# Two-layer diffusion step on one core: the first norm's loads and sums in another order, the next layer's adaLN sums held behind the second norm, a scratch tile of its own for the second layer's first norm, value weights in the key tiles' slots

## The chip, the cores and the metric

The kernel runs on one core of a Trainium2 chip. The metric is the device time of one execution in microseconds (us). Three timed runs of the kernel before gave a median of 1824.09 us (1818.67 to 1829.79). Smaller is better.

## The reference

One inference step of a two-layer flow-matching backbone on 128 context tokens and 512 latent tokens of width 1024. For each layer and each of the two token streams:

```
shift, scale, gate (x2) = SiLU(cond) @ w_ada[l] + b_ada[l]     # "adaLN": 6 x 1024 values per stream
h = rmsnorm(x, g_mix) * (1 + scale) + shift                    # first norm
p = h @ w_in[l]     # 14 x 128 columns of queries, keys, ropes, Fourier input, and 384 of values
o = latent attention, differential attention, Fourier mixing   # on the pieces of p
x = x + gate * (o @ w_out[l])
h = rmsnorm(x, g_ffn) * (1 + scale2) + shift2                  # second norm
x = x + gate2 * (conv_ffn(h, w_up, w_conv, w_down))
```

After the second layer a last rmsnorm gives the two outputs; keys, values and the compressed key cache are outputs too.

## The kernel before, in words

The activations lie transposed: 8 tiles `x_*` of 128 partitions (features) by 642 columns (128 context tokens, two of padding, 512 latent tokens). Matrix products run in fp32 precision as three passes: each operand is split into a high part (a cast on ScalarE, line 112) and a low part (a subtraction on VectorE or GpSimd, line 113), and `mm3` (lines 131 to 133) issues high x high, low x high and high x low. A weight comes by one DMA into a tile `raw` (two buffers, line 121) and is split into `whi` and `wlo`.

The stages, in order of time: `first` (line 895) loads x, sums its squares (`sq`, `acc`) and makes the reciprocal norms in `stats` (PSUM tile `rsh`, two token halves, each with a last step that copies `rb` and multiplies it by `ident`). `attention(0)` begins with `norm_first` (line 447): for k = 0 to 7 and for both halves `modulate` writes `nt` (VectorE), `hh` (ScalarE) and `hl` (VectorE, or GpSimd where a table says P), and TensorE multiplies them with the first two blocks of `w_in` into `pk` and `pq`. `diff_v` (line 465) follows: four blocks of the value weights times `hh`, `hl`; ahead of the third and the fourth, `warm(7, ...)` issues seven 512-column matmuls whose result nobody reads. Then come the heads in a written order, and `ffn(0)` (line 914): output projection `wo`, residual, second norm, and 22 pairs of `up` in three groups, each followed by a `down` (`dn`). The same again for layer 1, whose first-norm statistics come out of the last `down`: half 0 of the tokens has its last `down` first, then half 1.

The adaLN values of one column block (1024 inputs by 128 outputs; 48 a layer) are made in two ways. On TensorE, `sum_pe` (line 179): 8 matmuls, in the trace 16 passes, against `c_condT`, the SiLU of the condition in transposed form. On VectorE, `sum_dve` (line 156): two long multiply-and-sum instructions `junk<-ada,scond`, which read a weight column `ada` and the broadcast condition `scond`. The first norm of layer 0 needs columns 0 to 15: shifts in 0 to 7, scales in 8 to 15, so step k needs k and 8 + k. Columns 7, 14 and 15 go to VectorE, the other 13 to TensorE. A column waits for its tile: there is one slot for each of a few tags, and column 6 reuses a slot (`x32`) that another column held.

In `ffn(0)` a list of 56 columns (8 gates of layer 0, then the 48 of layer 1) goes to VectorE, three columns for each `up` pair. The program is written in plain order; a scheduler with priorities and a cost model then places each engine's instructions. In each engine's queue, SP's DMA queue among them, instructions start in the placed order, so one that waits holds all behind it.

Slots matter for three of the edits. `nt` has three buffers in `ffn`, released as each modulate ends. In `norm_first` of layer 1 `nt` is taken from attention's `rt` slots, which lie where `ffn`'s pools lay. `ks` (two buffers) holds a few adaLN columns early and the key tiles of the heads later.

Of the kernel before, what the change touches and what calls it, by code (L numbers as in the profile page):

```python
# [21 lines left out]
P = 128  # L22
L = 2
D = 1024
# [21 lines left out]
def backbone_kernel(ctx: ExitStack, tc: tile.TileContext, A, O):  # L46
# [7 lines left out]
    def tpt(nm):  # L54
        return gps.tile([P, 512], F32, name=nm, tag="tp", bufs=2)


    def const(name, shape):
        t = gp.tile(shape, F32, name="c_" + name)
        nc.sync.dma_start(out=t, in_=A[name])  # L60
        return t

    scT = const("condT", [P, NK, 2])
    nc.scalar.activation(out=scT, in_=scT, func=AF.Silu)
    bada = const("b_ada", [P, L, 48])
    gmix = const("g_mix", [P, L, NK])
    ident = gp.tile([P, P], F32, name="ident")
# [51 lines left out]
    def weight(src, n, lo_eng=None, pool=None, bufs=2, rpool=None):  # L119
        raw = raw_tile(rpool, 2 if rpool is None else 1)  # L120
        nc.sync.dma_start(out=raw[:, :n], in_=src)
        hi = (pool or gp).tile([P, 1024], F32R, name="whi", tag="whi", bufs=bufs)
        lo = (pool or gp).tile([P, 1024], F32R, name="wlo", tag="wlo", bufs=bufs)
        hi_lo(hi[:, :n], lo[:, :n], raw[:, :n], lo_eng)
        return hi, lo

    def on(c):
# [2 lines left out]
    def mm3(out, lh, ll, rh, rl, first, last):  # L130
        nc.tensor.matmul(out, lhsT=lh, rhs=rh, start=first, stop=False)  # L131
        nc.tensor.matmul(out, lhsT=lh, rhs=rl, start=False, stop=False)  # L132
        nc.tensor.matmul(out, lhsT=ll, rhs=rh, start=False, stop=last)  # L133


    def warm(n, lhsT, rhs):
        t = tpt("warm")[:, :rhs.shape[-1]]
        for _ in range(n):
            nc.tensor.matmul(t, lhsT=lhsT, rhs=rhs, start=True, stop=True)

    def h_tiles(l, tag):
        hh = [gp.tile([P, HW], F32R, name=f"hh{k}_{tag}{l}", tag=f"hh{k}") for k in range(NK)]
# [116 lines left out]
    def modulate(l, n, k, x, rb, hh, hl, pool, lo_pool=False):  # L259
        first = rb[0][0] == 0  # L260
        for t in (hh, hl):
            for z in ((0, 130) if first else (644,)):
                nc.gpsimd.memset(t[:, z:z + 2].bitcast(F32), 0.0)
        tt = pool.tile([P, 642], F32, name="nt", tag="t640")
        for o, w, c, r in rb:
            t = tt[:, o:o + w]
# [12 lines left out]

    def attention(l, xs, rb, close_x):  # L280
        with tc.tile_pool(name=f"at{l}", bufs=1, side="left", reuse_waits="tile") as ap, \
                tc.tile_pool(name=f"ap{l}", bufs=1, space=PSUM, reuse_waits="tile") as pp:

# [162 lines left out]

            def norm_first(before):
                get = lambda: [weight(A["w_in"][l, j], 1024) for j in range(2)]
                ws = get() if l else None
                ps = [sct("pk"), sct("pq")]  # L450
                for n in range(2 * NK):
                    hf, k = (n // NK, n % NK) if l else (n % 2, n // 2)
                    c0, w = PH[hf]
                    if l == 0 and hf == 0:
                        before(k)
                        ws = ws or get()
                    modulate(l, 0, k, xs[k], rb[hf], hh[k], hl[k], sm if l else Sm(t640), MOD_ENG[l][n] == "P")
                    s = slice(128 * k, 128 * k + 128)
                    r = slice(c0, c0 + w)
                    for (hi, lo), t in zip(ws, ps):  # L460
                        mm3(t[:, 512 * hf:512 * hf + w], hi[:, s], lo[:, s], hh[k][:, r], hl[k][:, r],
                            k == 0, k == NK - 1)
                return [[t[:, 512 * hf:512 * hf + w] for hf, (c0, w) in enumerate(PH)] for t in ps]

            def diff_v():
                vv = [vvt(f"VVd{p}") for p in range(NPAIR)]
                s0, s1, s2 = sct("vps0"), sct("vps1"), avt("vps2")
                ps = [s0[:, 0:384], s0[:, 512:896], s1[:, 0:384], s1[:, 512:896], s2[:, :384]]
                lo = None
                for i in range(4):  # L470
                    if i > 1:
                        warm(7, lo[:, :128], lo[:, :512])
                    hi, lo = weight(A["w_v"][l, i], 768)
                    for t in range(5):
                        for k in (2 * i, 2 * i + 1):
                            c0 = 132 + 128 * t if t < 4 else 2
                            s = slice(c0, c0 + 128)
                            w = slice(384 * (k % 2), 384 * (k % 2) + 384)
                            mm3(ps[t], hh[k][:, s], hl[k][:, s], hi[:, w], lo[:, w], k == 0, k == NK - 1)
                        if i == 3 and t < 4:  # L480
                            v_split(vv, t, ps[t])
# [298 lines left out]
            if l == 0:  # L780
# [17 lines left out]
                with later(-20000):  # L798
                    for j in (0, 8, 1, 9):
                        column(j, "w_ada0")  # L800

                def before(k):
                    if k == 0:
                        ada_cond(scond)
                        for j in ADA_V:
                            column(j, "w_adaT")
                    for j in (k, 8 + k):
                        if j in ADA_V:
                            sum_dve(0, j, cols[j], scond, junk)
                        else:  # L810
                            if j not in (0, 8, 1, 9):
                                column(j, "w_ada0")
                            sum_pe(j, cols[j], (avt if j < 8 else mmt)("adaps"))
                    make_gain(0, 0, k, k + 1)
            pk, pq = norm_first(before)
            close_x()
            xp = [tc.tile_pool(name=f"ax{l}", bufs=1, side="right", reuse_waits="tile")]
            xg = xp[0]
            xp[0] = xg.__enter__()
# [68 lines left out]
    def x_pool(nm):  # L888
# [4 lines left out]
        return xs, acc, lambda: g.__exit__(None, None, None)  # L893

    def first():
        xs, accs, close = x_pool("xin")

        class Pl:
            n = 0
# [12 lines left out]
        return xs, rb, close  # L912

    def ffn(l, oh, ol, ws):
        xs, accs, close = x_pool(f"x{l}")
        with tc.tile_pool(name=f"ff{l}", bufs=1, side="left", reuse_waits="tile") as fp, \
                tc.tile_pool(name=f"fps{l}", bufs=1, space=PSUM, reuse_waits="tile") as pf, ExitStack() as fpx:
            class Pl:
# [12 lines left out]
            def pst(nm):  # L931
                return pf.tile([P, 512], F32, name=nm, tag="f", bufs=6)

            def ada_list(js, xpool=None, engs=""):
                scond = ada_cond(fp.tile([P, 2, D], F32, name="scond", tag="scond"))
                junk = fp.tile([P, D], BF16, name="junk", tag="junk")
                if "P" in engs:
                    prod = xpool.tile([P, 2, D], F32, name="prod", tag="prod")

# [124 lines left out]
                make_gain(l + 1, 0)  # L1064
            down(f0, nf, [G[i] for i in range(f0, NFF)])
            if l + 1 < L:
                return xs, rb, close
        close()

    x = first()  # L1070
# [162 lines left out]
```

## Time and profile before

| what | us |
|---|---|
| median of three runs | 1824.09 |
| profiled execution, whole | 1816.04 |
| its span, first to last instruction | 1814.0 |
| TensorE busy in it | 1713.4 (94%) |
| VectorE busy | 1110.9 (61%) |
| ScalarE busy | 747.8 (41%) |
| GpSimd busy | 571.0 (31%) |

The profiled execution is 2.04 us longer than its span and lies 8.05 us (0.4%) under the median of the three runs. The mean granted TensorE clock is 0.968 of full speed. Times within the trace are counted from the span's start. In a row of the timeline the first number is the start, the second the length, and `[3.60 <-ACT whi L112]` says that the engine stood idle for 3.60 us before it, until ScalarE's line 112 wrote `whi`. A matmul's own length is longer than its share of the engine, since matmuls overlap: what counts is from start to next start.

### The profile page before, as it was taken

What the parts mean: (1) busy time and instruction counts of PE and PEld (TensorE: products, weight loads), DVE (VectorE), ACT (ScalarE), POOL (GpSimd) and SP (SyncE); (2) the same over time, 40 slices, a digit from 0 to 9 for tenths busy, and PEclk for the clock granted to TensorE, in tenths of its full rate; (3) what the DMA queues carried; (4) which work ended last, traced back from release to release, by engine and by line L of the source; (5) the groups of instructions that cost most, each with busy time, mean ns of one, the idle gap of its engine ahead of it and who ended that gap; (6) DMA issues with size and microseconds to landing.
All of it is one profiled execution on the core that took longest, in us unless ns stands there. A gap on an engine that the chain in (4) does not pass through costs nothing. (4 is left out here: it accounts for less than half of the span.)

```text
span 1814.0 us, 29499 instructions
## 1 busy us (share of the span) xinstructions
PE 1713.4 (94%) x11436; PEld 1671.0 (92%) x11436; DVE 1110.9 (61%) x2043; ACT 747.8 (41%) x1437; POOL 571.0 (31%) x691
## 2 busy tenths in 40 slices
PE   7888999998999999999999989989999999999997
PEld 6887899898999999999998878988999999999997
DVE  4538865678999996434462587675544434443445
ACT  4246665633333124313343566665343312331332
POOL 1356544424222102201324755552312200220122
PEclk8999899999899999999999989999999999999998
DMA  8467763675455662222247484643212222222223
GB/s 314 130 181 212 222 192 116 196 267 176 151 174 173 187 200 92 74 78 67 80 152 218 151 241 139 195 147 104 67 47 72 81 70 74 78 70 78 72 70 120
DMA packets 81355, 250.77 MB, mean 138 GB/s; under 512 B 10432, under 2 KB 19776, under 8 KB 79552
## 3 DMA queue, kind: packets, MB, share of 16 engines
q1 hardware_dynamic: 74496, 210.17, 36.3%
q0 software_dynamic: 6720, 38.72, 7.7%
q8 instruction: 90, 1.47, 0.3%
q14 instruction: 49, 0.40, 0.1%
HBM read 204.47 MB, written 41.24 MB: 135 GB/s over the span
## 5 line engine op out<-in xcount | busy, mean ns | idle before, releaser
L131 PE MATMUL up<-hh_o,whi 128*128 128x324 f32 x1408 | 439.6, 313 | 4.1 <-ACT hh_o L112 2.9
L133 PE MATMUL up<-hh_o,wlo 128*128 128x324 f32 x1408 | 440.4, 313 | 0.0
L132 PE MATMUL up<-hl_o,whi 128*128 128x324 f32 x1408 | 439.6, 312 | 0.0
L112 ACT CAST whi<-raw 128x1024 fp32r<-128x1024 f32 (+2 forms) x210 | 207.1, 990 | 420.2 <-PE dn L132 198.4
L113 DVE TENSOR_TENSOR wlo<-raw,whi 128x1024 fp32r<-128x1024 f32 (+2 forms) x184 | 227.2, 1238 | 215.7 <-ACT whi L112 203.9
L1016 POOL TENSOR_TENSOR cg<-cg,cv 128x644 f32<-128x644 f32 x44 | 76.5, 1739 | 660.2 <-DVE cv L1012 583.3
L131 PEld LDWEIGHTS up<-hh_o,whi 128*128 128x128 f32 x1408 | 267.0, 190 | 4.4 <-ACT hh_o L112 3.0
L132 PEld LDWEIGHTS up<-hl_o,whi 128*128 128x128 f32 x1408 | 267.3, 190 | 0.0
L133 PEld LDWEIGHTS up<-hh_o,wlo 128*128 128x128 f32 x1408 | 266.4, 189 | 0.0
L132 PE MATMUL dn<-gl,whi 128*128 128x322 f32 x704 | 219.3, 312 | 1.4 <-POOL gl L113 1.4
L131 PE MATMUL dn<-gh,whi 128*128 128x322 f32 x704 | 219.1, 312 | 1.1 <-ACT whi L112 1.1
L133 PE MATMUL dn<-gh,wlo 128*128 128x322 f32 x704 | 218.1, 311 | 0.0
L158 DVE CUSTOM_DVE_ANT_0 junk<-ada,scond 128x1024 bf16<-128x1024 f32 x134 | 174.4, 1301 | 4.9 <-ACT scond L149 2.5
L495 DVE TENSOR_REDUCE nm<-sc 128x1 f32<-128x640 f32 (+1 forms) x180 | 126.3, 710 | 68.3 <-PE sc L594 51.4
L496 ACT ACTIVATE P<-sc,nm 128x640 f32<-128x640 f32 (+1 forms) x180 | 128.3, 714 | 85.0 <-DVE nm L495 60.6
L885 DVE SCALAR_TENSOR_TENSOR x_x<-dn,mods,x_x 128x128 f32<-128x128 f32 (+2 forms) x144 | 58.4, 436 | 128.2 <-PE dn L133 128.2
L131 PEld LDWEIGHTS dn<-gh,whi 128*128 128x128 f32 x704 | 132.8, 189 | 3.0 <-ACT whi L112 2.7
L132 PEld LDWEIGHTS dn<-gl,whi 128*128 128x128 f32 x704 | 132.8, 189 | 1.9 <-POOL gl L113 1.8
L133 PEld LDWEIGHTS dn<-gh,wlo 128*128 128x128 f32 x704 | 132.8, 189 | 0.4 <-DVE wlo L113 0.4
L131 PE MATMUL proj<-hh_n,whi 128*128 128x320 f32 (+1 forms) x320 | 108.8, 340 | 2.8 <-ACT whi L112 1.0
L133 PE MATMUL proj<-hh_n,wlo 128*128 128x320 f32 (+1 forms) x320 | 105.9, 331 | 0.0
L113 DVE TENSOR_TENSOR tl<-tp,th 128x512 fp32r<-128x512 f32 x144 | 88.1, 617 | 28.2 <-ACT th L112 27.2
(297 smaller groups left out, 3608.3 us busy)
## 6 DMA issues: line engine op xcount, KB each, us to landing
raw<-in_w_up SPq DMA_DIRECT2D x88, 512.0 KB, 3.5
ada<-in_w_adaT SPq DMA_DIRECT2D x67, 512.0 KB, 3.9
raw<-in_w_down SPq DMA_DIRECT2D x32, 512.0 KB, 3.5
raw<-in_w_in SPq DMA_DIRECT2D x28, 512.0 KB, 5.1
raw<-in_w_down SPq DMA_DIRECT2D x32, 384.0 KB, 3.4
ada<-in_w_ada SPq DMA_DIRECT2D x21, 512.0 KB, 5.7
qs<-dq POOLq DMA_DIRECT2D x12, 865.5 KB, 8.4
ks<-mk POOLq DMA_DIRECT2D x12, 768.0 KB, 5.0
```

Of the source, the lines that this page charges most:

```text
L112: nc.scalar.copy(out=hi, in_=src)
L113: (lo_eng or nc.vector).tensor_tensor(out=lo, in0=src, in1=hi.bitcast(F32), op=ALU.subtract)
L131: nc.tensor.matmul(out, lhsT=lh, rhs=rh, start=first, stop=False)
L132: nc.tensor.matmul(out, lhsT=lh, rhs=rl, start=False, stop=False)
L133: nc.tensor.matmul(out, lhsT=ll, rhs=rh, start=False, stop=last)
L158: nc.vector.tensor_tensor_reduce(out=junk, in0=wt, in1=scond[:, c], op0=ALU.mult, op1=ALU.add, scale=1.0, scalar=0.0, accum_out=mods[:, l, ...
L495: nc.vector.tensor_reduce(out=nm, in_=s_in, axis=ax, op=ALU.max, negate=True)
L496: nc.scalar.activation(out=p_out, in_=s_in, func=AF.Exp, bias=nm, scale=1.0, accum_out=s_out)
L885: nc.vector.scalar_tensor_tensor(out=x[:, o:o + w], in0=ps, scalar=gate, in1=x[:, o:o + w], op0=ALU.mult, op1=ALU.add)
L1016: nc.gpsimd.tensor_tensor(out=c[0], in0=c[0], in1=c[1], op=ALU.mult)
```

## The change

There are six edits.

1. The load of `condT` and its SiLU are put ahead of everything.
2. In the first norm of layer 0 the two `w_in` blocks are loaded directly after x, and the adaLN columns are fetched in a written order, four at k = 0 (with `scond` among them) and three at each of k = 1 to 3. The VectorE sums of columns 14, 7 and 15 are issued at k = 1, 2 and 3.
3. `warm` and its two calls a layer are gone.
4. The value weights come as two DMAs of two blocks each into `ks` slots, after x is closed in layer 0 and before `norm_first` in layer 1, and are split from there; they no longer pass through `raw`.
5. In the list of 56 columns, the scratch `junk` (written and never read) takes an `nt` slot.
6. In layer 1, the first half of the first norm takes `nt` from a 322-column tile `scr` in the x pool (one buffer); the second half stays with `rt`.

```diff
+    tc.cur_priority -= 30000
     scT = const("condT", [P, NK, 2])
     nc.scalar.activation(out=scT, in_=scT, func=AF.Silu)
+    tc.cur_priority += 30000
...
-                ws = get() if l else None
+                ws = get()
...
-                    modulate(l, 0, k, xs[k], rb[hf], hh[k], hl[k], sm if l else Sm(t640), MOD_ENG[l][n] == "P")
+                    modulate(l, 0, k, xs[k], rb[hf], hh[k], hl[k], (scr, sm)[hf] if l else Sm(t640), MOD_ENG[l][n] == "P")
...
-                    if i > 1:
-                        warm(7, lo[:, :128], lo[:, :512])
-                    hi, lo = weight(A["w_v"][l, i], 768)
+                    hi, lo = split(wv[i // 2][:, i % 2], 768)
...
+                fetch = ((2, 10, -1, 14), (3, 11, 7), (4, 12, 15), (5, 13, 6))
+                sums = {1: 14, 2: 7, 3: 15}
+
                 def before(k):
-                    if k == 0:
-                        ada_cond(scond)
-                        for j in ADA_V:
-                            column(j, "w_adaT")
+                    for j in fetch[k] if k < len(fetch) else ():
+                        if j < 0:
+                            ada_cond(scond)
+                        else:
+                            column(j, "w_adaT" if j in ADA_V else "w_ada0")
                     for j in (k, 8 + k):
-                        if j in ADA_V:
-                            sum_dve(0, j, cols[j], scond, junk)
-                        else:
-                            if j not in (0, 8, 1, 9):
-                                column(j, "w_ada0")
+                        if j not in ADA_V:
                             sum_pe(j, cols[j], (avt if j < 8 else mmt)("adaps"))
+                    if k in sums:
+                        sum_dve(0, sums[k], cols[sums[k]], scond, junk)
                     make_gain(0, 0, k, k + 1)
+
+            def load_wv():
+                for i in range(2):
+                    t = ap.tile([P, 2, KW], F32, name="wv", tag="ks", bufs=2)
+                    nc.sync.dma_start(out=t, in_=A["w_v"][l, 2 * i:2 * i + 2].rearrange("i p n -> p i n"))
+                    wv.append(t)
+
+            wv = []
+            if l:
+                load_wv()
             pk, pq = norm_first(before)
             close_x()
+            if l == 0:
+                load_wv()
...
+        class Scr:
+            def tile(self, s, d, name, tag):
+                return p.tile([P, 322], d, name=name, tag="scr")
...
-                junk = fp.tile([P, D], BF16, name="junk", tag="junk")
+                if xpool:
+                    junk = xpool.tile([P, D], BF16, name="junk", tag="junk")
+                else:
+                    junk = fp.tile([P, 2 * 642], BF16, name="junk", tag="nt", bufs=FB["nt"])[:, :D]
```

What the scheduler makes of it, at three places. First the start of SP's DMA queue. Columns are `ada_*`; `in_w_ada` is the form for TensorE, `in_w_adaT` that for VectorE. Before:

```order
L60 DMA c_condT<-in_condT 128x16
...
L909 DMA x_xin<-in_xT 128x642 x8
L148 DMA scond<-in_cond 128x2x1024
L794 DMA ada_200<-in_w_adaT 128x1024
...
L121 DMA raw<-in_w_in 128x1024 x2
L794 DMA ada_323<-in_w_ada 128x1024
...
L121 DMA raw<-in_w_v 128x768 x2
L794 DMA ada_490<-in_w_ada 128x1024
L794 DMA ada_502<-in_w_ada 128x1024
L794 DMA ada_545<-in_w_ada 128x1024
```

And now:

```order
L60 DMA c_condT<-in_condT 128x16
L790 DMA ada_189<-in_w_ada 128x1024 x2
...
L925 DMA x_xin<-in_xT 128x642 x8
L123 DMA raw<-in_w_in 128x1024 x2
L790 DMA ada_210<-in_w_ada 128x1024
L790 DMA ada_212<-in_w_ada 128x1024
L147 DMA scond<-in_cond 128x2x1024
L790 DMA ada_216<-in_w_adaT 128x1024
...
L123 DMA raw<-in_w_in 128x1024 x2
L790 DMA ada_392<-in_w_ada 128x1024
L790 DMA ada_394<-in_w_ada 128x1024
L818 DMA wv<-in_w_v 128x2x768 x2
L790 DMA ada_396<-in_w_ada 128x1024
```

The first two `w_in` blocks moved ahead of `scond` and the columns. The last column (`ada_396`, column 6) now stands behind two more `w_in` blocks and both loads of value weights.

Second, VectorE around the second norm of layer 0, from the mean `ms` of the second half to the first `nt`. `x_x` is the residual stream, `cg` a step of the first `up`. Before:

```order
L244 TENSOR_SCALAR ms<-rsh 128x3
L1012 SCALAR_TENSOR_TENSOR cg<-up,wconv,cg 128x322
L158 ISA junk,mods<-ada,scond 128x1024
L158 ISA mods 128x1
L249 COPY rb<-rs 128x384
L161 TENSOR_SCALAR mods<-mods,c_b_ada 128x2
L158 ISA junk,mods<-ada,scond 128x1024
...
L267 SCALAR_TENSOR_TENSOR nt<-x_x_4326,gain,rsh 128x320
```

And now:

```order
L243 TENSOR_SCALAR ms<-rsh 128x3
L1032 SCALAR_TENSOR_TENSOR cg<-up,wconv,cg 128x322
L248 COPY rb<-rs 128x384
L267 SCALAR_TENSOR_TENSOR nt<-x_x_4306,gain,rsh 128x320
L267 SCALAR_TENSOR_TENSOR nt<-x_x_4307,gain,rsh 128x320
```

The sums are gone from here; the first of them now stands behind the last `nt` of this norm. Further on they stand three to a `wlo`, as before, for some six weights longer.

Third, TensorE where layer 1 begins: the end of the last `dn` and the statistics of the second half (`rsh`). Before:

```order
L133 MATMUL dn<-gh,wlo 128x322
L241 MATMUL rsh<-ones,acc_x_5194 128x1
L241 MATMUL rsh<-ones,sq 128x1
...
L252 MATMUL rsh<-ident,rb 128x128 x2
L252 MATMUL rsh<-ident,rb 128x65
L131 MATMUL pk<-hh_n_9848,whi 128x320
L131 MATMUL pq<-hh_n_9848,whi 128x320
```

And now:

```order
L138 MATMUL dn<-gh,wlo 128x322
L240 MATMUL rsh<-ones,acc_x_5174 128x1
L136 MATMUL pk<-hh_n_9828,whi 128x320
L137 MATMUL pk<-hl_n_9836,whi 128x320
...
L240 MATMUL rsh<-ones,sq 128x1
L240 MATMUL rsh<-ones,acc_x_5174 128x1
...
L136 MATMUL pk<-hh_n_9833,whi 128x320
...
L251 MATMUL rsh<-ident,rb 128x128 x2
L251 MATMUL rsh<-ident,rb 128x65
L136 MATMUL pk<-hh_n_9835,whi 128x320
```

Of the 48 first-half products, 17 now stand between the first and the second statistics matmul, 25 more ahead of the last step (`rb`), and 6 behind it, ahead of the second half.

Besides these, rows move through the whole attention of layer 0 on all engines, because its schedule is made anew from another start; attention of layer 1 keeps nearly all of its order.

## Rows read from the trace of the kernel before

**Rows 1.** Windows: length, busy PE, PEld, DVE, ACT, POOL, PEclk, DMA share, GB/s.

```profile
0.00:20.00 20.00, 11.22 (x85) 11.22 (x86) 6.25 (x18) 9.33 (x11) 2.56 (x50) 1.00 0.93 355
20.00:40.00 20.00, 15.50 (x100) 15.09 (x100) 11.00 (x31) 8.42 (x17) 5.40 (x15) 0.74 0.98 348
```

**Rows 2.** Timeline of TensorE, first norm of layer 0.

```profile
27.07 0.64 PE L131 MATMUL pk<-hh_n,whi 128*128 128x320 f32 x1 [3.60 <-ACT whi L112]
...
35.23 5.52 PE L182 MATMUL adaps<-c_condT,ada 128*128 128x128 f32 x48
...
60.23 0.64 PE L131 MATMUL pk<-hh_n,whi 128*128 128x320 f32 x1 [3.23 <-ACT hh_n L275]
...
62.57 0.63 PE L132 MATMUL pk<-hl_n,whi 128*128 128x320 f32 x1 [1.43 <-DVE hl_n L276]
...
67.89 0.31 PE L133 MATMUL pq<-hh_n,wlo 128*128 128x322 f32 x1
```

**Rows 3.** Tile `junk`, VectorE's sums, from 40 to 66 and 427 to 470 us.

```profile
L158 DVE CUSTOM_DVE_ANT_0 junk<-ada,scond x6: 1211/1214/1217, 53.0 to 62.4; 128x1024 bf16<-128x1024 f32 x6
...
L158 DVE CUSTOM_DVE_ANT_0 junk<-ada,scond x19: 1210/1216/1777, 429.0 to 468.1; 128x1024 bf16<-128x1024 f32 x19
```

**Rows 4.** Timeline of TensorE in `diff_v` of layer 0, one of four such places.

```profile
81.49 1.78 PE L139 MATMUL warm<-wlo 128*128 128x512 f32 x7
83.11 0.34 PE L131 MATMUL vps<-whi,hh_n 128*128 128x384 f32 x1
```

**Rows 5.** Timeline of TensorE, second norm of layer 0.

```profile
442.80 0.30 PE L133 MATMUL wo<-hh_o,wlo 128*128 128x320 f32 x1
...
447.12 0.38 PE L241 MATMUL rsh<-ones,acc_x 128*128 128x1 f32 x2 [2.39 <-POOL acc_x L231]
...
454.16 1.54 PE L252 MATMUL rsh<-ident,rb 128*128 128x128 f32 x6 [3.61 <-DVE rb L249]
458.56 0.91 PE L131 MATMUL up<-hh_o,whi 128*128 128x324 f32 x2 [2.86 <-ACT hh_o L112]
```

**Rows 6.** Timeline of GpSimd there.

```profile
442.86 1.93 POOL L231 TENSOR_TENSOR acc_x<-acc_x,sq 128x320 f32<-128x320 f32 x1
...
446.21 0.86 POOL L231 TENSOR_TENSOR acc_x<-acc_x,sq 128x320 f32<-128x320 f32 x1
```

**Rows 7.** Timeline of TensorE, second norm of layer 1.

```profile
1315.51 0.31 PE L133 MATMUL wo<-hh_o,wlo 128*128 128x320 f32 x1
...
1324.53 0.91 PE L131 MATMUL up<-hh_o,whi 128*128 128x324 f32 x2 [1.24 <-ACT hh_o L275]
```

**Rows 8.** Timeline of TensorE, first norm of layer 1.

```profile
934.39 0.28 PE L241 MATMUL rsh<-ones,acc_x 128*128 128x1 f32 x2
935.91 0.38 PE L241 MATMUL rsh<-ones,sq 128*128 128x1 f32 x2 [1.24 <-ACT sq L229]
...
938.97 1.54 PE L252 MATMUL rsh<-ident,rb 128*128 128x128 f32 x6 [1.78 <-DVE rb L249]
...
957.78 0.30 PE L133 MATMUL pq<-hh_n,wlo 128*128 128x322 f32 x1
```

**Rows 9.** Timeline of VectorE, first norm of layer 1: the first half's `rb`, the first `nt`.

```profile
917.64 0.55 DVE L249 COPY rb<-rs 128x384 f32<-128x384 f32 x1 [0.97 <-POOL rs L247]
...
938.83 1.25 DVE L267 SCALAR_TENSOR_TENSOR nt<-x_x,gain,rsh 128x128 f32<-128x128 f32 x4
```

**Rows 10.** Windows: layer 1's norm, both attentions, and `ffn(0)`.

```profile
937.00:944.00 7.00, 5.22 (x22) 5.14 (x22) 5.80 (x20) 2.94 (x9) 1.01 (x5) 0.53 0.27 66
...
68.00:443.00 375.00, 350.23 (x2409) 333.46 (x2408) 248.22 (x491) 203.21 (x457) 187.80 (x229) 0.97 0.63 199
958.00:1316.00 358.00, 329.96 (x2154) 311.57 (x2154) 222.95 (x427) 193.70 (x441) 179.10 (x217) 0.95 0.53 160
...
500.00:580.00 80.00, 80.00 (x539) 80.00 (x538) 80.00 (x134) 25.50 (x40) 20.34 (x10) 1.00 0.56 171
700.00:780.00 80.00, 80.00 (x540) 80.00 (x539) 37.35 (x58) 26.43 (x38) 15.83 (x10) 1.00 0.26 80
```

More of the change, by code (lines that the diff above doesn't have):

```diff
@@ L121, in weight, with split @@
         nc.sync.dma_start(out=raw[:, :n], in_=src)
+        return split(raw[:, :n], n, lo_eng, pool, bufs)
+    def split(raw, n, lo_eng=None, pool=None, bufs=2):
         hi = (pool or gp).tile([P, 1024], F32R, name="whi", tag="whi", bufs=bufs)
         lo = (pool or gp).tile([P, 1024], F32R, name="wlo", tag="wlo", bufs=bufs)
-        hi_lo(hi[:, :n], lo[:, :n], raw[:, :n], lo_eng)
+        hi_lo(hi[:, :n], lo[:, :n], raw, lo_eng)
         return hi, lo
@@ L133, in mm3 @@
         nc.tensor.matmul(out, lhsT=ll, rhs=rh, start=False, stop=last)
[L136 to L139, printed above, removed]
     def h_tiles(l, tag):
@@ L264, in modulate @@
         tt = pool.tile([P, 642], F32, name="nt", tag="t640")
+        o0 = 0 if tt.shape[-1] > 322 else rb[0][0]
         for o, w, c, r in rb:
-            t = tt[:, o:o + w]
+            t = tt[:, o - o0:o - o0 + w]
             nc.vector.scalar_tensor_tensor(out=t, in0=x[:, o:o + w], scalar=gain[:, l, n, k, c:c + 1],
@@ L277, in modulate, with attention @@
                                            op0=ALU.add, op1=ALU.subtract)
-    def attention(l, xs, rb, close_x):
+    def attention(l, xs, rb, close_x, scr=None):
         with tc.tile_pool(name=f"at{l}", bufs=1, side="left", reuse_waits="tile") as ap, \
@@ L455, in norm_first @@
                         before(k)
-                        ws = ws or get()
-                    modulate(l, 0, k, xs[k], rb[hf], hh[k], hl[k], sm if l else Sm(t640), MOD_ENG[l][n] == "P")
+                    modulate(l, 0, k, xs[k], rb[hf], hh[k], hl[k], (scr, sm)[hf] if l else Sm(t640), MOD_ENG[l][n] == "P")
                     s = slice(128 * k, 128 * k + 128)
@@ L468, in diff_v @@
                 ps = [s0[:, 0:384], s0[:, 512:896], s1[:, 0:384], s1[:, 512:896], s2[:, :384]]
-                lo = None
                 for i in range(4):
-                    if i > 1:
-                        warm(7, lo[:, :128], lo[:, :512])
-                    hi, lo = weight(A["w_v"][l, i], 768)
+                    hi, lo = split(wv[i // 2][:, i % 2], 768)
                     for t in range(5):
@@ L892, in x_pool @@
         acc = lambda: p.tile([P, TW], F32, name="acc_" + nm, tag="acc")
-        return xs, acc, lambda: g.__exit__(None, None, None)
+        class Scr:
+            def tile(self, s, d, name, tag):
+                return p.tile([P, 322], d, name=name, tag="scr")
+        return xs, acc, lambda: g.__exit__(None, None, None), Scr()
     def first():
-        xs, accs, close = x_pool("xin")
+        xs, accs, close, _ = x_pool("xin")
         class Pl:
@@ L914, in ffn @@
     def ffn(l, oh, ol, ws):
-        xs, accs, close = x_pool(f"x{l}")
+        xs, accs, close, scr = x_pool(f"x{l}")
         with tc.tile_pool(name=f"ff{l}", bufs=1, side="left", reuse_waits="tile") as fp, \
@@ L1066, in ffn @@
             if l + 1 < L:
-                return xs, rb, close
+                return xs, rb, close, scr
         close()
```

## The prediction

> **What bounds the kernel now.** I read the table of busy times first: TensorE works nearly all of the time, so the kernel can gain only where TensorE idles, runs at half clock, or does work that nobody needs. Then I went through TensorE's timeline for its idle spots and the wait that ends last at each, and through the windows for the granted clock. Four places answer to the edits.
>
> The start: DMA moves 355 and 348 GB/s in the first two windows of 20 us, its engines 93% and 98% busy [rows 1]: a stage bound by loads. TensorE waits 3.60 us for the first `w_in` block's cast (ScalarE's line 112), and near the end of the norm 3.23 and 1.43 us for `hh` and `hl` [rows 2]. What stands ahead of these on VectorE are six sums of 1.21 us, between 53.0 and 62.4 us [rows 3].
>
> `diff_v`: seven filler matmuls take 83.11 − 81.49 = 1.62 us [rows 4].
>
> The second norm of layer 0: from the last `wo` to the first `up` of the second half it takes 458.56 − 442.80 = 15.76 us, with 2.39, 3.61 and 2.86 us of idle TensorE [rows 5]. 19 sums of 1.22 us lie on VectorE between 429.0 and 468.1 us [rows 3]. Layer 1 has the same step without sums, in 1324.53 − 1315.51 = 9.02 us [rows 7].
>
> The first norm of layer 1: 1.24 and 1.78 us idle around the statistics [rows 8]. The first half's `rb` was ready at 917.64, but its first `nt` starts only at 938.83 [rows 9], since `rt` lies where `ffn`'s pools still live. The clock is 0.53 in the 7 us there [rows 10]: almost all at 1.2 rather than 2.4 GHz, about 3.4 us lost.
>
> **The start (edits 1 and 2).** TensorE's needs, from the first product on: nine columns at 5.52/3 = 1.84 us [rows 2] are 16.6 us, and 96 products at 80.00/539 = 0.148 us [rows 10] are 14.2, together 30.8. It takes 40.8 us, from 27.07 to 67.89 [rows 2]; 4.7 of these are the two idle spots, and the 5.3 left over I put down to half clock (0.74 granted in the second window [rows 1]). With `w_in` early, the first product can start when the first `hh` is there, about 25 us; and one and a half columns (2.8 us) now stand ahead of it in TensorE's order. If one stretch of half clock stays (3 us), TensorE would end at 25 + 28.0 + 3 = 56. The loads: 16 columns of 0.524 MB, x 2.63, four `w_in` blocks 2.10, value weights 1.57, `scond` 1.05 and about 0.8 MB of constants (sizes from the code) make 16.5 MB, all ahead of or with column 6; at 350 GB/s [rows 1] it lands at 47 to 48. Behind it come 1.84 us of sums, three VectorE and ScalarE steps (about 3) and 12 products (1.8): 54.6. So neither bound is far from the other. I add 2 us of waiting: 58 in place of 68, **a gain of 10**. The upper end is 13 (end at 55, loads alone); the lower is 4, if the last column is as late as now and only the 3.60 us go. The six sums move into k = 1 to 3, where VectorE is busy 11.00 of 20 us [rows 1]: room for their 7.3 us, but no more than that. `condT` first costs one small DMA ahead of the columns: nothing, since the loads set the pace.
>
> **No fillers (edit 3), value weights by `ks` (edit 4).** Four times 1.62 us [rows 4] are **6.5**. The cover that makes it whole: a block lasts 30 products of 384 columns, some 5 us at 0.148 for 324 columns [rows 10], and the next block is loaded already, so only its cast and subtraction must fit in there. If TensorE waited as long as the fillers lasted, the gain would be 0. The two loads of value weights are two DMAs in place of four, and wait in SP's order for `ks` slots, with column 6 behind them; that is in the 48 us above. In layer 1 they wait for `ffn`'s pools, some 20 us ahead of their use: nothing.
>
> A rule speaks against this edit. The trace shows at 937 to 944 that a stretch after two idle spots runs at a clock of 0.53 [rows 10]. The Trainium skill, "TensorE: Matmul & The Clock Gate", section "HAM oscillation — how this bites in real kernels", says that a loop whose compute is shorter than the wait for its next weights falls to the slow clock on each turn. By that rule the fillers would be what holds the clock, and edit 3 would lose rather than gain; it is a rival below. I take the trace's side, since products stand directly before and behind the fillers.
>
> **The second norm of layer 0 (edit 5).** With the sums gone the step should look like layer 1's: 15.76 − 9.02 = 6.7 us [rows 5, 7], the upper end. It may keep GpSimd's chain: its last `acc` begins at 446.21 [rows 6], and TensorE's statistics wait for it. If that stays, only what follows goes: after the wait of 2.39 us, 3.61 + 2.86 = 6.47 us of idling [rows 5] against about 2.4 in layer 1 without sums (twice 1.24 [rows 7] as a bound), so 4.1. I take **5.5**.
>
> For that choice: one of GpSimd's additions took 1.93 us beside sums, its like 0.86 without [rows 6]. The Trainium skill, "SBUF — State Buffer", section "SBUF: two separate sides", says that a VectorE operation with two SBUF inputs and a GpSimd operation lock each other out of a shared port. By it GpSimd would end earlier too and the gain go to 5.2 or more; without it, 4.1.
>
> The 19 sums (23 us) must go behind the norm. There VectorE is full, 80.00 of 80 us, beside a TensorE that is full too; from 700 on it is busy 37.35 of 80 [rows 10]. They take that room, at the same three per weight, so I cost them at nothing; if that cover fails, see the last rival.
>
> **The first norm of layer 1 (edit 6).** 25 + 17 products now fill the 3.0 us of idling [rows 8] and make the half-clock stretch (3.4 us [rows 10]) unlikely: 6.4 is the upper end. But the last step of the second half's statistics now stands behind those products, 42 × 0.148 = 6.2 us after 934.39 and 1.5 us of statistics, at 942; the second half's eight pairs of `nt` and `hl` follow on VectorE, each instruction some 0.55 us as the 384-column copy [rows 9], and end at about 952, the products at 953, against 958 [rows 8]. **Gain 4.5.** Lower end 0: `scr` is one buffer, so each k waits for the one before, and VectorE holds the last `wlo` and residuals meanwhile.
>
> **The attention of layer 0**, whose order is made anew. The trace holds two schedules of this work: 375 us in layer 0, less eight gate columns of 1.84 [rows 2] = 360.3, and 358 in layer 1 [rows 10]. They differ by 2.3. I take 0, within ±5.
>
> **Sum:** 10 + 6.5 + 5.5 + 4.5 = 26.5 us off the profiled execution of 1816.04, that is 1789.5. That execution lies 8.05 us under the median of the runs, so the forecast is 1824.09 − 26.5 = 1797.6 us.
>
> **Rivals.**
>
> *Half of it.* The start is DMA-bound still, column 6 comes late behind the value weights (4 in place of 10), GpSimd keeps its chain (4.1), and VectorE's order eats the gain at layer 1's norm (0): 4 + 6.5 + 4.1 = 14.6, so 1809.5. For it: column 6 is last in SP's order. Against: TensorE has 30 us of other work until then.
>
> *The clock falls without fillers* (the rule above). Each of four places waits as long as the filler took and loses 3.4 us at half clock [rows 10]: −13.6 in place of +6.5. 1824.09 − 20 + 13.6 = 1817.7. Against: the weights are there.
>
> *The new order gives it back.* Layer 0's attention loses about five stretches of half clock (3.4 each [rows 10]) with an idle spot of 1.2 each (as [rows 8]): 5 × 4.6 = 23, so 1821. Against: the two schedules agree within 2.3 us.
>
> *Slower: VectorE becomes the bound of `ffn(0)`.* It is already full beside TensorE [rows 10]; 23 us more of sums would each delay `wlo` or the reading of PSUM. Price: 23 us of waiting, and with it half clock for some six weights, 3.4 each: 43 us, less 26.5: 1841. It decides once the loss passes 26.5 + 9 us. Against: the same three sums per weight stood there before and TensorE did not wait.
>
> **How the numbers follow.** About 0.5%, 9 us, is what a measurement of this kernel can tell from no change: 1815 to 1833. Chances: the forecast 0.60; half of it 0.23; the clock 0.05; no gain 0.06; slower 0.06. Faster: 0.60 + 0.23 = 0.83. Same: 0.05 + 0.06 = 0.11. Slower 0.06. Range: below, all upper ends (13 + 6.5 + 6.7 + 6.4 = 32.6), 5 from the attention and 2.5 for the spread of the runs: 1784. Above, the half case with 4 us of the attention's 5: 1814.
>
> **What would show it.** The start: the last product of the first norm at 55 to 60 us, no wait for `whi`, column 6 landing by 50; wrong if it ends past 63. `diff_v`: no idle spot over 0.5 us between blocks, clock at full. Second norm of layer 0: 9 to 11 us from the last `wo` to `up`, GpSimd's addition at 0.9. First norm of layer 1: no idle spot around the statistics, end 4 to 6 us after less. `ffn(0)`: sums until about 710 us, TensorE still without waits. The forecast is wrong if TensorE idles in `ffn(0)`, or if attention of layer 0 grows by more than 5 us.

## The result, and the profile after

The changed kernel takes 1795.59 us (median of 4 runs, 1790.54 to 1797.75), the kernel before 1822.71 (4 runs): a ratio of 0.9852, with a 95% interval of 0.9823 to 0.9881. That is 27.1 us less; 26.5 were forecast, 1797.6 us. The profiled executions, 1816.04 and 1793.88 us, differ by less, 22.2 us, because that of before was shorter than all four of its timed runs. The stages below are read from them; their spans, from the first instruction to the last, are 1814.0 and 1792.1 us.

| stage, by TensorE's starts (us) | before | after | moved | forecast |
|---|---|---|---|---|
| start to the last product of layer 0's first norm | 67.89 | 62.07 | −5.8 | −10 |
| `diff_v`, layer 0 (first to last `vps`) | 27.24 | 23.47 | −3.8 | −3.2 |
| attention, layer 0 (last `vps` to last `wo`) | 346.9 | 347.5 | +0.6 | 0 |
| second norm, layer 0 (last `wo` to `up`) | 15.76 | 10.12 | −5.6 | −5.5 |
| `ffn(0)` from there to the last `dn` | 475.7 | 475.7 | 0.0 | 0 |
| first norm, layer 1 (last `dn` to last product) | 23.53 | 19.57 | −4.0 | −4.5 |
| `diff_v`, layer 1 | 28.03 | 23.46 | −4.6 | −3.2 |
| attention, layer 1 | 328.9 | 329.6 | +0.7 | 0 |
| the rest: the two steps into `diff_v`, and all behind layer 1's last `wo` | | | +0.6 | 0 |
| sum, which is what the spans differ by | | | −21.9 | −26.5 |

The start, on TensorE's timeline of the changed kernel (start, length, then the idle time before it and what ended it):

```profile
5.05 10.18 PE L181 MATMUL adaps<-c_condT,ada 128*128 128x128 f32 x64 [5.05 <-DMA ada<-in_w_ada]
19.08 0.59 PE L240 MATMUL rsh<-ones,acc_xin 128*128 128x1 f32 x2 [3.85 <-DVE acc_xin L230]
...
25.85 3.92 PE L181 MATMUL adaps<-c_condT,ada 128*128 128x128 f32 x24
29.61 0.78 PE L251 MATMUL rsh<-ident,rb 128*128 128x128 f32 x6
30.20 0.39 PE L136 MATMUL pk<-hh_n,whi 128*128 128x320 f32 x1
...
45.78 0.41 PE L137 MATMUL pk<-hl_n,whi 128*128 128x320 f32 x1 [1.67 <-DVE hl_n L276]
...
62.07 0.30 PE L138 MATMUL pq<-hh_n,wlo 128*128 128x322 f32 x1
```

ScalarE, the first `hh`:

```profile
26.48 0.78 ACT L275 ACTIVATE hh_n<-nt,mods 128x128 fp32r<-128x128 f32 x2 [7.15 <-DVE nt L267]
```

The waits of [rows 2] are gone; one of 1.67 us and three under 0.7 us stand elsewhere. But the first product comes at 30.20, later than before (27.07): ahead of it stand the statistics and 24 passes of column sums at 3.92/24 = 0.163 us, where [rows 2] had 5.52/48 = 0.115. The first `hh` is there at 27.3, when ScalarE's two instructions end. The windows show the clock of that stretch (length, busy time of PE, PEld, DVE, ACT, POOL, then PEclk, DMA share, GB/s):

```profile
17.75:27.99 10.24, 8.76 (x40) 8.67 (x41) 5.95 (x12) 2.86 (x5) 3.25 (x14) 0.50 1.03 410
...
920.00:927.00 7.00, 5.98 (x43) 5.98 (x44) 6.46 (x16) 4.15 (x10) 2.03 (x6) 1.00 0.68 224
...
500.00:580.00 80.00, 78.90 (x530) 78.64 (x529) 80.00 (x135) 25.56 (x41) 16.27 (x10) 1.00 0.52 170
700.00:780.00 80.00, 79.59 (x535) 79.32 (x534) 48.17 (x77) 23.50 (x34) 15.92 (x10) 1.00 0.31 100
```

0.50, which is half clock, from 17.75 to 27.99 us, so from inside the idle spot ahead of the statistics; 1.00 behind the last `dn`, against 0.53 in [rows 10]. In the last two rows VectorE is full for longer, as the held sums had to go somewhere, and TensorE lacks 1.1 and 0.4 us of 80.

SP's queue, from the value weights to column 6:

```profile
40.29 2.46 SPq L818 DMA_DIRECT2D wv<-in_w_v  x2
49.34 0.34 SPq L790 DMA_DIRECT2D ada<-in_w_ada  x1
```

Column 6 is issued at 49.34, 6.6 us after the value weights. It does not wait for bandwidth but for the slot that column 5 holds, until TensorE has summed that column (SP's waits from 0 to 64 us: line, what it waited for, us in total, times, the longest):

```profile
SPq L790 <- PE adaps L181: 7.2, 3, 6.5
```

The two later norms, on TensorE's timeline, in answer to [rows 5] and [rows 8]:

```profile
433.69 0.30 PE L138 MATMUL wo<-hh_o,wlo 128*128 128x320 f32 x1
...
435.47 0.28 PE L240 MATMUL rsh<-ones,acc_x 128*128 128x1 f32 x2
...
440.58 1.19 PE L251 MATMUL rsh<-ident,rb 128*128 128x128 f32 x6 [1.79 <-DVE rb L248]
443.81 0.91 PE L136 MATMUL up<-hh_o,whi 128*128 128x324 f32 x2 [2.04 <-ACT hh_o L114]
...
919.47 0.30 PE L138 MATMUL dn<-gh,wlo 128*128 128x322 f32 x1
...
921.02 0.38 PE L240 MATMUL rsh<-ones,acc_x 128*128 128x1 f32 x2 [1.24 <-POOL acc_x L230]
...
928.68 0.78 PE L251 MATMUL rsh<-ident,rb 128*128 128x128 f32 x6
...
939.04 0.31 PE L138 MATMUL pq<-hh_n,wlo 128*128 128x322 f32 x1
```

In layer 0 the wait for GpSimd's `acc` is gone. The wait for `rb`, 1.79 us, has the size of that in layer 1 before (1.80); the one for `hh_o`, 2.04, is longer than layer 1's 1.24 [rows 7]. GpSimd itself, in answer to [rows 6]:

```profile
431.79 0.88 POOL L230 TENSOR_TENSOR acc_x<-acc_x,sq 128x320 f32<-128x320 f32 x1 [2.69 <-ACT sq L228]
```

It has idle time now, and this last addition starts before the last `wo`. In layer 1 the last step of the statistics (928.68) has no idle spot ahead of it; one of 1.24 us stays, at 921.02.

### The profile page after: what moved, and what is told of

Read it like the earlier page. It is cut to its first block, busy times and chain, and to the rows that moved or that the text cites. A ratio compares the mean times of both kernels' runs of the same rounds, so it can differ in the third digit from the quotient of the medians.

```text
span 1792.1 us, 29413 instructions
## 1 busy us (share of the span) xinstructions
PE 1705.8 (95%) x11408; PEld 1663.8 (93%) x11408; DVE 1116.4 (62%) x2043; ACT 745.7 (42%) x1437; POOL 561.0 (31%) x691
## 5 line engine op out<-in xcount | busy, mean ns | idle before, releaser
L114 ACT CAST whi<-raw 128x1024 fp32r<-128x1024 f32 (+2 forms) x202 | 200.3, 996 | 390.9 <-PE dn L137 183.1
L115 DVE TENSOR_TENSOR wlo<-raw,whi 128x1024 fp32r<-128x1024 f32 (+2 forms) x176 | 212.3, 1209 | 179.6 <-ACT whi L114 177.3
L1036 POOL TENSOR_TENSOR cg<-cg,cv 128x644 f32<-128x644 f32 x44 | 71.3, 1621 | 671.3 <-DVE cv L1032 621.9
L137 PE MATMUL proj<-hl_n,whi 128*128 128x320 f32 (+1 forms) x320 | 103.5, 323 | 0.0
```

The source lines that it names most:

```text
L114: nc.scalar.copy(out=hi, in_=src)
L115: (lo_eng or nc.vector).tensor_tensor(out=lo, in0=src, in1=hi.bitcast(F32), op=ALU.subtract)
L1036: nc.gpsimd.tensor_tensor(out=c[0], in0=c[0], in1=c[1], op=ALU.mult)
```

## The experiments

All but the first are told by the stage that they touch and by the attentions. Each ran once with a profile.

**The same kernel again.**

> The changed kernel once more, word for word. It tells how far a stage's time differs between two executions of one order. Theory (the order decides): each stage within 1 us of the first execution: attention of layer 0 (last value product to last wo) 347.5, of layer 1 329.6, first norm of layer 0 ends near 62. Rival (chance of the execution): the attentions differ by 5 us or more, as they did between the kernels with one edit undone (344.9 to 363.3 in layer 0, 328.2 to 335.9 in layer 1).

1794.75 us. The first norm ends at 61.65, attention takes 346.7 and 331.1; no stage differs by more than 1.5 us from the first execution, which for attention of layer 1 is more than the 1 us expected. Other runs below happen to hold the same orders, and widen the bound. Layer 0's attention stands in one order on all engines in the changed kernel, here and without edit 6: 347.5, 346.7 and 344.9 us. On TensorE and VectorE layer 1's stands in one order in the kernel before, the changed one, here and with the fillers back: 328.9, 329.6, 331.1 and 328.2. The first norm of layer 0 stands in one order in the changed kernel, here, without edit 5, without edit 6 and with the fillers back, and ends at 62.07, 61.65, 61.90, 60.38 and 61.67. So one order varies by up to 3 us in an attention and 1.7 us in the first norm; larger differences of these three stages came only with another order.

**Edit 5 undone.**

```diff
-                if xpool:
-                    junk = xpool.tile([P, D], BF16, name="junk", tag="junk")
-                else:
-                    junk = fp.tile([P, 2 * 642], BF16, name="junk", tag="nt", bufs=FB["nt"])[:, :D]
+                junk = fp.tile([P, D], BF16, name="junk", tag="junk")
```

> The changed kernel with edit 5 alone undone: the scratch of the held sums has a slot of its own again. Theory: the 5.64 us gained at the second norm of layer 0 (last wo to the first up of the second half: 15.76 us before, 10.12 in the changed kernel) come from the held sums alone. Then that step is 15 to 16 us again, the rest of the stages within 0.7 us of the changed kernel, span 1797 to 1798. Rival: the step is shorter because the new order of attention leaves GpSimd and VectorE ahead when the norm begins; then it stays at 10 to 12 us without the hold.

1803.86 us; the second norm of layer 0 takes 16.00 us. TensorE's timeline there:

```profile
434.95 0.30 PE L138 MATMUL wo<-hh_o,wlo 128*128 128x320 f32 x1
...
439.88 0.38 PE L240 MATMUL rsh<-ones,acc_x 128*128 128x1 f32 x2 [1.96 <-POOL acc_x L230]
...
446.56 1.54 PE L251 MATMUL rsh<-ident,rb 128*128 128x128 f32 x6 [4.28 <-DVE rb L248]
450.96 0.91 PE L136 MATMUL up<-hh_o,whi 128*128 128x324 f32 x2 [2.86 <-ACT hh_o L114]
```

All three waits are back, GpSimd's too. The gain is the held sums' alone. The "within 0.7 us" was wrong of three stages: attention of layer 1 took 334.4, 4.8 more, in another order of instructions; attention of layer 0 took 1.4 more and `ffn(0)` 1.0 less. So the span is 1802.1, not 1797 to 1798.

**Edit 6 undone.**

```diff
-                    modulate(l, 0, k, xs[k], rb[hf], hh[k], hl[k], (scr, sm)[hf] if l else Sm(t640), MOD_ENG[l][n] == "P")
+                    modulate(l, 0, k, xs[k], rb[hf], hh[k], hl[k], sm if l else Sm(t640), MOD_ENG[l][n] == "P")
```

> The changed kernel with edit 6 alone undone: both halves of layer 1's first norm take nt from attention's slots. Theory: the norm (last dn to last product of pk, pq: 23.54 us before, 19.57 in the changed kernel) is 23 to 24 us again, with idle spots of 1.2 and 1.8 us around the statistics and a clock near half in the 7 us behind them. Rival: what helped there is that the w_in blocks and value weights are loaded earlier; then it stays at 19 to 21 us.

1800.51 us; the first norm of layer 1 takes 23.53 us, as before. Its TensorE timeline, and the window of 7 us there:

```profile
915.26 0.31 PE L138 MATMUL dn<-gh,wlo 128*128 128x322 f32 x1
916.93 0.38 PE L240 MATMUL rsh<-ones,sq 128*128 128x1 f32 x2 [1.24 <-ACT sq L228]
...
919.98 1.12 PE L251 MATMUL rsh<-ident,rb 128*128 128x128 f32 x6 [1.78 <-DVE rb L248]
```

```profile
918.00:925.00 7.00, 5.22 (x25) 4.82 (x26) 5.79 (x20) 2.92 (x9) 1.01 (x5) 0.76 0.87 295
```

The theory holds of the time and the idle spots: the scratch is worth 4.0 us. It was wrong of the clock, 0.76 where near half was expected (0.53 before [rows 10]). Since the norm takes 23.53 us with either, the part of the half clock that is gone had cost nothing.

**Fillers put back.**

```diff
+                lo = None
                 for i in range(4):
+                    if i > 1:
+                        warm(7, lo[:, :128], lo[:, :512])
                     hi, lo = split(wv[i // 2][:, i % 2], 768)
```

> The changed kernel with the fillers put back (28 matmuls in four places), value weights still from the ks slots. diff_v takes 23.5 us in either layer without them (27.2 and 28.0 before). Theory: each filler group costs its 1.62 us, so diff_v is 26.7 in either layer, span about 1798.6, clock as without. Rival by the clock: the fillers hold the clock; then diff_v or the attention behind it wins half-clock stretches of 3.4 us back and the span grows by less than 3 us or falls.

1804.69 us; `diff_v` takes 26.69 and 26.71 us, 3.2 more in either layer. So the fillers hold no clock there: beside value weights from `ks` they are pure cost in this stage. The span grew by 10.8 us, not 6.5, with 2.4 more in attention of layer 0 and 3.6 more in `ffn(0)`.

**Fillers taken out of the kernel before, nothing else.**

```diff
-                    if i > 1:
-                        warm(7, lo[:, :128], lo[:, :512])
```

> The kernel before with the fillers alone taken out; value weights still pass through raw. Theory: the fillers cost 1.62 us each wherever they stand and hid nothing, so diff_v falls from 27.2 and 28.0 us to 24.0 and 24.8, clock as before. Rival: with raw's two buffers the third and fourth blocks come late, TensorE waits for them as long as the fillers lasted and the clock falls to half behind the wait; then diff_v stays at 27 us or more.

1839.17 us, slower than before (1825.07 beside it); `diff_v` takes 28.25 and 29.91 us: longer without 3.2 us of fillers than with them. That is 2.9 us of the slowdown; most of the rest lies in attention of layer 0, 358.4 us. TensorE near the end of layer 0's `diff_v`:

```profile
95.57 0.45 PE L131 MATMUL vps<-whi,hh_n 128*128 128x384 f32 x1 [3.67 <-DVE VVd L444]
...
98.41 0.53 PE L132 MATMUL vps<-wlo,hh_n 128*128 128x384 f32 x1
98.73 0.53 PE L133 MATMUL vps<-whi,hl_n 128*128 128x384 f32 x1
```

The `VVd` that it waits for hang on ScalarE, whose timeline shows why they are late, with SP's issue of the load below:

```profile
83.49 0.84 ACT L112 CAST whi<-raw 128x768 fp32r<-128x768 f32 x1 [0.71 <-PE vps L133]
92.74 1.04 ACT L112 CAST whi<-raw 128x1024 fp32r<-128x1024 f32 x1 [8.41 <-DMA raw<-in_w_in]
93.69 0.26 ACT L443 CAST VVd<-vps 128x128 fp32r<-128x128 f32 x1
```

```profile
80.18 3.26 SPq L835 DMA_DIRECT2D mk<-x  x4
83.54 1.10 SPq L121 DMA_DIRECT2D raw<-in_w_in  x1
```

The cast of the next `w_in` block stands ahead of the casts of `VVd` in ScalarE's order, and waits 8.41 us for its load. That load needs a slot of `raw`, which a value weight held until its split ended at 80.42 us; it was issued at 83.54, behind four `mk` transfers, and the cast starts at 92.74. With the fillers, in the kernel before, ScalarE waits as long, and TensorE only 0.56 us:

```profile
91.05 1.05 ACT L112 CAST whi<-raw 128x1024 fp32r<-128x1024 f32 x1 [8.53 <-DMA raw<-in_w_in]
```

```profile
93.88 0.44 PE L131 MATMUL vps<-whi,hh_n 128*128 128x384 f32 x1 [0.56 <-DVE VVd L444]
```

So the rival was right that the fillers hid a wait, and wrong on which: it is not the third and fourth block, but what stands behind them.

**Edits 3 and 4 on the kernel before.** The diff is these two edits' part of the change.

> The kernel before with edits 3 and 4 together: no fillers, value weights through the ks slots. Without fillers alone diff_v took 28.25 and 29.91 us, since TensorE waited 3.67 and 4.81 us for the last blocks' split, behind a cast on ScalarE that waited for the next w_in block in raw. Theory: the fillers covered that load, and edit 4 removes the wait by leaving raw free; then diff_v is 23.4 to 23.6 us in both layers, as in the changed kernel, with no idle spot over 0.5 us inside. Rival: the changed kernel's diff_v is short because its earlier start of norm and w_in loads left the queue ahead; then diff_v stays at 25 us or more here.

`diff_v` takes 23.47 and 23.46 us, with no idle spot over 0.5 us inside: the theory holds. The cast of the next `w_in` block waits for no load any more, but for a value product:

```profile
87.58 1.05 ACT L112 CAST whi<-raw 128x1024 fp32r<-128x1024 f32 x1 [4.45 <-PE vps L136]
```

Edit 4 takes the wait away, and edit 3 collects it. The kernel as a whole took 1827.99 (before beside it: 1818.03), since attention came out at 358.9 and 333.9. That a different place for the cast in ScalarE's order would do as well was not tried.

**Edit 1 undone.**

```diff
-    tc.cur_priority -= 30000
     scT = const("condT", [P, NK, 2])
     nc.scalar.activation(out=scT, in_=scT, func=AF.Silu)
-    tc.cur_priority += 30000
```

> The changed kernel with edit 1 alone undone: condT is loaded behind the first four columns again. In the changed kernel TensorE starts its first columns at 5.05 us, ends them at 15.23, then idles 3.85 us until the statistics at 19.08, which run at half clock (0.60 granted from 20 to 30 us); the first product stands at 30.20. Theory: the early start makes that idle spot, so without it the columns end near 18, the idle spot is 1 us or less, the clock stays at full over the statistics, the first product comes at 26 to 28 and the norm ends at 58 to 61 rather than 62.07. Rival: the late sums of squares on VectorE, and not condT, set the statistics and the clock falls anyway; then the norm ends at 62 or later.

1819.38 us; the norm ends at 63.80. TensorE's timeline, and two windows:

```profile
9.82 9.82 PE L179 MATMUL adaps<-c_condT,ada 128*128 128x128 f32 x64 [9.82 <-DMA x_xin<-in_xT]
19.47 0.50 PE L238 MATMUL rsh<-ones,acc_xin 128*128 128x1 f32 x4
...
22.40 3.76 PE L179 MATMUL adaps<-c_condT,ada 128*128 128x128 f32 x16
```

```profile
15.00:21.70 6.70, 6.70 (x63) 6.70 (x61) 5.00 (x13) 4.18 (x5) 0.47 (x9) 1.00 1.03 411
21.70:28.50 6.80, 6.80 (x33) 6.80 (x33) 3.61 (x8) 0.75 (x3) 2.98 (x8) 0.50 1.03 399
```

My theory fell, and the rival's numbers came: the statistics stand at 19.47, the first product at 30.24. TensorE has no idle spot from 9.82 to 31 us, and yet the 16 passes behind the statistics take 3.76 us, 0.235 each. The clock falls to half at 21.7, 2.2 us into the statistics, where in the changed kernel it fell at 17.75, in the idle spot. So taking the idle spot away did not keep the clock up; what makes it fall here was not taken apart. Edit 1, costed at nothing in the prediction, is worth 1.7 us by this one run against the changed kernel, and 3.4 against the shortest run of that order. Both theories priced the norm alone; most of the 25 us lost lie in the attentions, 363.3 and 335.7.

**Column 6 in a slot that is free early.**

```diff
-tag, n, b = ("VV", 6 * 256, NPAIR) if j in ADA_V else
+tag, n, b = ("VV", 6 * 256, NPAIR) if j in ADA_V or j == 6 else
```

> The changed kernel with one thing more: column 6 gets a slot that is free early, so it is loaded ahead of the value weights and waits for no other column's sum (it was issued at 49.34 us). Theory: TensorE was already behind when the column came (idle 0.3, 0.7 and 0.2 us only from 52 us on), so the norm ends at 60.5 to 62 rather than 62.07. Rival (the end is set by the loads): the norm ends 4 us earlier, at 58.

1812.25 us; the norm ends at 61.44, inside the theory's range and far from the rival's. That is 0.6 earlier than in the changed kernel and within the 60.38 to 62.07 of its order, so no gain is shown. The late load of column 6 does not set the end. Attention took 358.3 and 334.7.

**x first.** Column 6 as above, and:

```diff
+    tc.cur_priority -= 25000
     x = first()
+    tc.cur_priority += 25000
```

> The changed kernel with x loaded and its squares summed ahead of the first four columns, and column 6 in a slot that is free early. The changed kernel's first product came at 30.20 us, since the statistics began at 19.08 and ran at half clock with 24 column passes behind them. Theory (the late statistics are what the start lost): the statistics begin at 12 to 14, the first product comes at 24 to 27, and the norm ends at 56 to 59. Rival (TensorE's sums are the limit, wherever the statistics stand): four columns of 1.84 us move from under the loads of x to behind them, the first product comes no earlier than 28 and the norm ends at 61 or later. Whatever the norm does, the attention's order is made anew and may take 10 us more or less.

1804.13 us; the norm ends at 65.08. TensorE's timeline:

```profile
12.30 1.01 PE L240 MATMUL rsh<-ones,acc_xin 128*128 128x1 f32 x4 [12.30 <-DVE acc_xin L230]
...
17.44 3.76 PE L181 MATMUL adaps<-c_condT,ada 128*128 128x128 f32 x16
...
22.91 6.92 PE L181 MATMUL adaps<-c_condT,ada 128*128 128x128 f32 x60
29.58 0.39 PE L136 MATMUL pk<-hh_n,whi 128*128 128x320 f32 x1
```

The statistics begin 6.8 us earlier, and the first product comes 0.6 us earlier: the rival holds. 80 column passes now stand between the statistics and the first product, where 24 stood. The sums of the first columns are in the way wherever the statistics stand. Attention of layer 0 took 363.5, of layer 1 321.6, the shortest seen.

**Edits 1 and 2 undone.** The diff is their part of the change, taken back.

> The changed kernel with edits 1 and 2 undone: the first norm of layer 0 loads and sums in the order of before. Theory: the 5.8 us gained there come from these two edits; the norm ends at 67 to 70 again, the other named stages stay as in the changed kernel (diff_v 23.5, second norm 9.8 to 10.5, first norm of layer 1 19.6). The attention's order is made anew: 345 to 364 us in layer 0, 322 to 336 in layer 1. Rival: the value weights' loads alone set the end; then it stays at 62 to 65.

1816.69 us; the norm ends at 68.36, and the other named stages stay: 23.47, 9.81, 19.57, 23.47. The 5.8 us are these edits'. The four runs that hold the start of before end it at 67.89, 69.69, 68.49 and 68.36, the five of the new order at 60.38 to 62.07: by their means the two edits gain 7.1 us. Attention took 359.8 and 333.4, 12.2 and 3.8 more than in the changed kernel.

**What the attentions show together.** The same work in twelve executions:

| | layer 0 | layer 1 |
|---|---|---|
| before; changed; the same again | 346.9; 347.5; 346.7 | 328.9; 329.6; 331.1 |
| without edit 5; without 6; fillers back | 349.0; 344.9; 350.0 | 334.4; 335.9; 328.2 |
| without 1; column 6; x first | 363.3; 358.3; 363.5 | 335.7; 334.7; 321.6 |
| before: no fillers; with edits 3 and 4 | 358.4; 358.9 | 331.1; 333.9 |
| without 1 and 2 | 359.8 | 333.4 |

Layer 0 comes in two groups, 345 to 350 and 358 to 364. In layer 1 the order of the kernel before takes 328 to 331 us; another, the same on all engines without edit 1, with column 6 moved and with edits 3 and 4 on the kernel before, takes 335.7, 334.7 and 333.9. The window from 150 to 190 us shows a good one (changed) and then a bad one (without edit 1):

```profile
150.00:190.00 40.00, 34.53 (x219) 30.88 (x218) 33.41 (x63) 26.12 (x61) 22.49 (x19) 0.91 0.81 235
```

```profile
150.00:190.00 40.00, 30.44 (x166) 27.14 (x165) 32.62 (x54) 20.89 (x51) 18.85 (x18) 0.83 0.64 189
```

TensorE is busy 4.1 us less of 40, and at a lower clock: the bad order idles more and pays for it twice. Its longest waits in about that stretch, and below them that of the changed kernel at the same step (engine and line, what it waited for: us in total, times, the longest):

```profile
PE sc L582 <- ACT P L490: 3.5, 3, 2.7
PE sc L585 <- ACT P L490: 2.9, 4, 1.3
```

```profile
PE sc L587 <- ACT P L492: 1.3, 2, 1.1
```

Scores wait for ScalarE's softmax, 6.4 us in all against 1.3. But this does not part the groups: over the whole stage these waits are 11.8 us without edit 1 and 6.3 in the changed kernel, yet 5.8 without edits 1 and 2, which is a bad order too. Which of the moved instructions makes an order good or bad stays open; it was not tried.

## Why the prediction was right, by its own steps

**The total** came out within 2 us of the forecast, by medians. By the profiles the four terms of 26.5 us measured 23.8 together, the start 4.2 short and `diff_v` 1.8 over, and the spans differ by 21.9. The agreement of the medians is better than that of the terms, and to that extent luck.

**The start was mis-sized:** 10 forecast, 5.8 measured. The step that failed is "the first product can start when the first `hh` is there, about 25 us". It came at 30.20. The statistics began at 19.08, 1.3 us later than in the kernel before (17.75), which is chance: in the five executions of the new order they begin at 18.01 to 19.08. They ran at half clock (0.50 from 17.75 to 27.99 us). So the first `hh` was there at 27.3 and not at 25, and TensorE came to the product only at 30.20, since the 24 column passes, at 0.163 us each, and the last step of the statistics stood ahead of it. From there 28.0 us of work were forecast and 31.9 passed, with 3.9 of waits and slack, where I had allowed 3 for half clock and 2 for waiting. The "one stretch of half clock" that I allowed 3 us for was there, but ahead of the first product, where I had counted none of it. By the means of all runs with either start the gain is 7.1, still short of 10. The loads' bound (column 6 at 47 to 48) did not decide: that column was issued only at 49.34, for its slot, and giving it another one moved the end by no more than one order varies by.

**`diff_v` gained more, 8.3 against 6.5, and for a reason that I had only half.** I wrote that the cover is the next block, loaded already. The fillers covered something else: a `w_in` load that waits for `raw`, and a cast ahead of the ones that TensorE needs. Without edit 4 the edit would have cost 1.0 and 1.9 us a layer where I forecast a gain. Edit 4, which I priced as two DMAs in place of four, is what made the 6.5 possible; its own 1.8 us are the idle spots of 0.56 and 1.36 us at the same place that had stayed in spite of the fillers. The rule of the Trainium skill ("TensorE: Matmul & The Clock Gate", section "HAM oscillation — how this bites in real kernels") that I set aside is borne out on the kernel before without its fillers, in a small way: behind the wait of 3.67 us the last value products start 0.32 us apart (98.41, 98.73) where the changed kernel has 0.18 (86.00, 86.18), and 28.25 − 3.67 − 23.47 = 1.1 us of the stage is that. It took one wait at the end, not one for each block. In the changed kernel nothing waits there, so the rule asks for nothing.

**The second norm** gained 5.6 against 5.5, and the sums were its whole cause. GpSimd's chain, which I had kept as the lower end, went too; the addition beside a sum fell from 1.93 to 0.88 us, as the Trainium skill ("SBUF — State Buffer", section "SBUF: two separate sides") would have it. With the sums back one takes 1.84 us beside a sum that starts 0.16 us ahead of it. The total hides two errors that cancel: the waits for `rb` and `hh_o` gave 2.6 us where I had counted 4.1, and GpSimd's gave its whole 2.39. The held sums cost little in `ffn(0)`: they end at 713 us, and the stage takes 475.7 as before, 474.6 with the sums not held. I had written that the forecast is wrong if TensorE idles there; it waits once for VectorE, 1.1 us. So the slower rival did not come.

**Layer 1's first norm** gained 4.0 against 4.5. The delay that I charged to the last step of the statistics is in the trace: 928.68, 9.2 us behind the last `dn`, where it stood 4.7 us behind it before. One idle spot of 1.24 us stayed. The 3.4 us of half clock that I had put into the upper end are not borne out: without edit 6 about half of them were gone, and the norm took as long as before.

**The attention** was right at 0 and wrong in its bounds. ±5 came from two placements that lay 2.3 us apart; others of the same work lie up to 16.6 us away in layer 0 and 7.3 in layer 1. The changed kernel fell into the good group, as the kernel before had; nothing in my argument assured that. Had it not, the gain would have been some 11 to 16 us: 27.1 less the 10.8 to 16.0 by which the bad group lies above the changed kernel's 347.5.

## What to carry to other kernels

A filler on the busy engine may be covering a wait that this engine's own timeline hardly shows while it runs (0.56 us here, with 8.53 us on ScalarE): before taking it out, look at what the other engines have queued up behind it, and free that first. Where a scheduler places the instructions, an edit's own stage tells its worth; the total also holds what the new order does elsewhere, here up to 16 us, so judge by stages and repeat one order to know the noise. An engine's earliest start on a step is not set by its first operand alone: count what its own order puts ahead, at the clock that it will have there.

## What had not been expected of the hardware

The granted clock fell while TensorE showed no idle time: without edit 1 it worked from 9.82 us on without a spot, and in and behind 24 single-column matmuls, from 19.47 to 22.4 us, the clock fell to half (0.50 from 21.70 to 28.50 us) and the column passes took 0.235 us each, where 0.115 is full speed [rows 2]. Busy time in the profile did not keep it at 2.4 GHz. That the narrow matmuls were the cause is not shown: no run changed them alone.
